# Fifteen early input blocks in place of nine in a two-layer transformer step

## The chip, the cores and the metric

The kernel runs on one core of one Trainium2 chip. The metric is the device time of one execution in microseconds (us), the median over several runs. The core has TensorE for matmuls (with a separate row for its weight loads), VectorE, ScalarE, GpSimd, and SyncE, whose queue issues plain transfers; 16 DMA engines move the data.

## The reference

The program applies two blocks to a sequence of 512 tokens of width 1024, all in float32. The first block mixes tokens by attention branches and then applies a PEER layer: for each token 128 experts are chosen, a row of `peer_u` and a row of `peer_v` (1024 numbers each) is fetched per expert, and the output is a weighted sum of the `peer_v` rows. The second block is a sparse attention and a feed-forward with a short causal convolution. Cut to what matters here:

```python
def peer_ffn(h, w_q, keys1, keys2, u_tab, v_tab):
    ...                                    # expert (128 per token), gate
        u = u_tab[eb]
        act = jax.nn.gelu(jnp.einsum('td,ted->te', hb, u), approximate=False)
        v = v_tab[eb]
        return jnp.einsum('te,ted->td', gb * act, v)

def conv_ffn(h, w_in, conv_w, conv_b, w_out):     # w_in: 1024 x 5632, D_FF = 2816
    u, v = jnp.split(h @ w_in, 2, axis=-1)
    u = conv(u, conv_w) + conv_b                  # causal, 3 taps along the sequence
    return (jax.nn.gelu(u, approximate=False) * v) @ w_out

def second_block(x, c, ...):
    ...
        x = x + gt_m * dsa_mixer(h, ...)
        h = rmsnorm(x, g_ffn[i]) * (1 + sc_f) + sh_f
        x = x + gt_f * conv_ffn(h, ...)
    return rmsnorm(x, g_final)
```

## The kernel before

The 512 tokens are four tiles of 128, numbered 0 to 3. The first block's attention part is done for tiles 0 and 1 and then 2 and 3. After that come, per tile, the PEER layer `peer(ti)` and the second block: its attention `dsa(t0, nt)`, and its feed-forward, `ffn_mod` (norm and modulation), `ffn_in` and `ffn_out`.

`peer(ti)` issues 128 gathers of `peer_u` rows (512 KB each: 128 tokens x 4 KB) from GpSimd (L618), a dot product on VectorE for each (L632), then 128 gathers of `peer_v` rows and a multiply-add on VectorE for each (L649). The rows use eight buffers in turn. One load of `ffn_norm_w` goes through SyncE into such a row buffer as well (L628).

The feed-forward's 2816 columns are 22 blocks of 128. One input block (`ffn_in`, L938 to L960) loads two 512 KB weight tiles through SyncE (L88, four buffers shared with `ffn_out`), multiplies them into two PSUM banks (L944, tag "mm", three banks), copies and convolves on ScalarE and VectorE (L947 to L954), and multiplies the halves into `gv` (L956). The cost in columns of a matmul is the number of tokens, 128 a tile; the weights are loaded anew for every pass over a block. The convolution needs the last two tokens of the tile before, kept in `fhalo`, so a block's tiles go in order.

The order of the work is set by priorities: a planner orders each engine's instructions once, when the program is built, by priority (mostly the order in the source) as their inputs and buffers come free. At run time each engine, and SyncE's queue, takes its instructions in that order. The lines around the change are L993 to L1015: attention of tiles 0 and 1 beside `peer(2)`; then, for tiles 0 and 1, the modulation and the first `EARLY` = 9 input blocks (256 columns); then the attention of tile 2, which needs `peer(2)`; then the first nine blocks for tile 2 alone (128 columns), the other 13 for tiles 0 to 2 together (384 columns), `ffn_out` of the three tiles (L978, three banks "mm"); `peer(3)` beside these at a lower place; the attention of tile 3 with a raised one; the feed-forward of tile 3, and `finish` (the last norm and the store, L986).

Of the kernel before, what the change touches and what calls it, by code (L numbers as in the profile page):

```python
# [26 lines left out]
LOW = -1e37  # L27
MARK = -3e38
GROUPS = ((0, 2, True), (2, 2, False))
EARLY = 9  # L30
LAG = 1
SPANS = [(a, sum(16 // (i + 1) for i in range(a)), 16 // (a + 1)) for a in range(8)]
NCAND = 50
# [26 lines left out]
def build(nc, tc, A, out):  # L60
# [872 lines left out]
    def ffn_in(F, t0, nt, fs):  # L933

        i0, _, hT, gv = F
        n = nt * 128
        cs = tok(t0 - i0, nt)
        for f in fs:  # L938
            bs = []
            for half in range(2):  # L940
                b = bank()[:, :n]
                w = w3(A["f_w_in"][half * NF + f], 8, tag="wf")
                for k in range(8):
                    PE.matmul(b, w[:, k, :], hT[:, k, cs], start=k == 0, stop=k == 7)  # L944
                bs.append(b)
            xb = sb.tile([128, NFG + 2], F32, name="xbf", bufs=2)[:, :n + 2]
            SC.activation(xb[:, 0:2], fhalo[:, f, :], AF.Copy)  # L947
            SC.activation(xb[:, 2:], bs[0], AF.Copy)
            SC.activation(fhalo[:, f, :], xb[:, n:n + 2], AF.Copy)
            y = sf("yf")[:, :n]  # L950
            SC.activation(y, xb[:, 0:n], AF.Copy, scale=fcw[:, f, 0:1])
            for c in (1, 2):
                V.scalar_tensor_tensor(y, xb[:, c:c + n], fcw[:, f, c:c + 1], y, op0=OP.mult, op1=OP.add)
            SC.activation(y, y, AF.Gelu, bias=fcw[:, f, 3:4])  # L954
            if len(gv) == 1:
                V.tensor_tensor(gv[0][:, f, cs], bs[1], y, op=OP.mult)  # L956
            else:
                V.tensor_tensor(y, bs[1], y, op=OP.mult)
                SC.activation(gv[0][:, f, cs], y, AF.Copy)
                V.tensor_tensor(gv[1][:, f, cs], y, gv[0][:, f, cs].bitcast(F32), op=OP.subtract)  # L960

    def ffn_mod(F, t0, nt):
        for ti in range(t0, t0 + nt):
            mod_T(ti, cols[4], cols[3], F[2][:, :, tok(ti - F[0])], "mm")

    def ffn_out(F):
        t0, nt, _, gv = F
        for q in range(2):
            qs = slice(q * 512, (q + 1) * 512)
            bs = [bank() for _ in range(nt)]  # L970
            for k0 in range(0, NF, 2):
                src = A["f_w_out"][q][:, k0 * 512:(k0 + 2) * 512]
                w = w3(src, 2, tag="wf") if len(gv) == 1 else wsplit(src, 2)
                for i in range(nt):
                    for k in range(2):
                        first, last = k0 + k == 0, k0 + k == NF - 1
                        if len(gv) == 1:
                            PE.matmul(bs[i], gv[0][:, k0 + k, tok(i)], w[:, k, :], start=first, stop=last)  # L978
                        else:
                            mm3(bs[i], [g[:, k0 + k, tok(i)] for g in gv], [t[:, k, :] for t in w], None, first, last)  # L980
            for i in range(nt):
                t = sf("yo")
                V.tensor_tensor(t, bs[i], gts[5][:, qs], op=OP.mult)
                V.tensor_tensor(x[:, t0 + i, qs], x[:, t0 + i, qs], t, op=OP.add)
# [13 lines left out]
    ffn_mod(F, 0, 2)  # L998
    ffn_in(F, 0, 2, range(EARLY))
    dsa(2, 1)  # L1000
    p0 = tc.cur_priority
    ffn_mod(F, 2, 1)
    ffn_in(F, 2, 1, range(EARLY))
    ffn_in(F, 0, 3, range(EARLY, NF))
    ffn_out(F)
# [105 lines left out]
```

## Time and profile before

| | us |
|---|---|
| median of 3 runs | 2645.74 |
| range of the runs | 2644.31 to 2646.25 |
| profiled execution | 2659.27 |
| its span in the trace | 2657.5 |
| TensorE matmul busy | 2075.4 (78%) |
| VectorE busy | 1983.3 (75%) |
| GpSimd busy | 1182.3 (44%) |
| ScalarE busy | 830.5 (31%) |

The profile is of one execution. Its first part gives busy times, its second cuts the span into 40 slices of 66.4 us, its fourth is the chain of work that ended last, its fifth the costliest groups of instructions. Other answers of the trace give busy times by stretch, instructions by line, the timeline and the transfers. Busy shares are means over stages with different limits, so a stage is read by its own rows.

### The profile page before, as it was taken

To read this page: it belongs to the slowest core of one execution; us is meant where nothing else is said; L and a number is where in the kernel's file an instruction comes from. 1 tells how busy PE (TensorE), PEld (TensorE's weight loads), DVE (VectorE), ACT (ScalarE), POOL (GpSimd) and SP (SyncE) were. 2 spreads that over 40 slices of the span, in tenths; PEclk is the share of its full clock that TensorE was granted. 3 is DMA by queue.
4 is the path that set the end of the run, shared out by engine and by line. 5 is a ranking of instruction groups with operands and counts; after the bars stand their busy time and mean duration, and the time that the engine had idled before them with its cause. 6 is when DMAs were issued, how large, how long until landed. Compare 5 with 4: busy or idle time off the path is not lost. (4 is left out here: it accounts for less than half of the span.)

```text
span 2657.5 us, 31631 instructions
## 1 busy us (share of the span) xinstructions
PE 2075.4 (78%) x10438; PEld 1572.0 (59%) x10438; DVE 1983.3 (75%) x4068; ACT 830.5 (31%) x1827; POOL 1182.3 (44%) x1092
## 2 busy tenths in 40 slices
PE   5988999888987899886766655658053789898997
PEld 5887889577776677764622234637032565444795
DVE  6873333289799999778899589887989778875235
ACT  5655563223344344111211123411022221003444
POOL 0111100024656877555566755665765557860000
PEclk9999999998999999898899967879566999999999
DMA  8852335368979799999998999999999999992286
GB/s 272 280 174 67 95 105 184 118 241 315 372 284 339 261 358 387 386 409 406 404 325 307 356 390 372 350 381 407 400 384 339 399 409 409 395 409 87 80 287 235
DMA packets 230596, 808.85 MB, mean 304 GB/s; under 512 B 26617, under 2 KB 34081, under 8 KB 230433
## 3 DMA queue, kind: packets, MB, share of 16 engines
q0 software_dynamic: 147456, 536.94, 53.1%
q1 hardware_dynamic: 82976, 269.90, 28.5%
q8 instruction: 83, 1.36, 0.2%
q14 instruction: 81, 0.66, 0.1%
HBM read 802.52 MB, written 4.21 MB: 304 GB/s over the span
## 5 line engine op out<-in xcount | busy, mean ns | idle before, releaser
L618 POOL DMA_INDIRECT row<-peer_u,exi x512 | 489.6, 956 | 682.2 <-DVE ix L552 269.2
L618 POOL DMA_INDIRECT row<-peer_v,exi x512 | 609.7, 1191 | 245.1 <-issue 102.8
L632 DVE CUSTOM_DVE_ANT_0 row<-row,h 128x1024 f32<-128x1024 f32 x512 | 613.6, 1213 | 78.8 <-DMA row<-peer_u,exi 77.8
L649 DVE SCALAR_TENSOR_TENSOR x<-row,pw,x 128x1024 f32<-128x1024 f32 x448 | 584.7, 1305 | 83.1 <-DMA row<-peer_v,exi 77.6
L944 PE MATMUL bmm<-hTf,w 128*128 128x128 f32 (+2 forms) x1696 | 317.3, 347 | 19.7 <-DMA w<-f_w_in 9.4
L944 PEld LDWEIGHTS bmm<-hTf,w 128*128 128x128 f32 x1696 | 246.4, 191 | 89.9 <-DVE gv L956 10.1
L271 PE MATMUL bmm<-hT,w 128*128 128x256 f32 x1168 | 273.9, 385 | 2.9 <-ACT xb L307 1.3
L271 PEld LDWEIGHTS bmm<-hT,w 128*128 128x128 f32 x1168 | 221.6, 193 | 42.7 <-issue 10.0
L647 PE MATMUL acc<-row,dgw 128*128 128x512 f32 x256 | 130.2, 636 | 81.4 <-DMA row<-peer_v,exi 67.6
L351 POOL TENSOR_TENSOR Lb<-LT,clevels_b 128x512 f32<-128x512 f32 x56 | 71.0, 1271 | 268.9 <-DVE LT L342 209.3
L99 DVE TENSOR_TENSOR wrowb<-w,wrowa 128x1024 fp32r<-128x1024 f32 x95 | 118.3, 1250 | 76.8 <-ACT wrowa L98 76.7
L105 PE MATMUL bmm<-hTh,wrowa 128*128 128x256 f32 x584 | 169.8, 292 | 2.9 <-ACT hTh L209 2.8
L106 PE MATMUL bmm<-hTl,wrowa 128*128 128x256 f32 x584 | 170.9, 293 | 0.7 <-DVE hTl L210 0.7
L107 PE MATMUL bmm<-hTh,wrowb 128*128 128x256 f32 x584 | 168.6, 289 | 0.8 <-DVE wrowb L99 0.8
L647 PEld LDWEIGHTS acc<-row,dgw 128*128 128x128 f32 x256 | 45.6, 197 | 165.3 <-issue 90.5
L978 PE MATMUL bmm<-w,gv 128*128 128x512 f32 x264 | 118.8, 604 | 10.3 <-DVE gv L956 8.6
L98 ACT ACTIVATE wrowa<-w 128x1024 fp32r<-128x1024 f32 x95 | 100.3, 1058 | 81.7 <-PE bmm L106 36.3
L271 PE MATMUL bmm<-h2T,w 128*128 128x256 f32 x512 | 120.6, 390 | 0.0
L105 PEld LDWEIGHTS bmm<-hTh,wrowa 128*128 128x128 f32 x584 | 111.8, 192 | 5.8 <-ACT hTh L209 3.2
L106 PEld LDWEIGHTS bmm<-hTl,wrowa 128*128 128x128 f32 x584 | 111.5, 191 | 4.5 <-issue 3.1
L107 PEld LDWEIGHTS bmm<-hTh,wrowb 128*128 128x128 f32 x584 | 111.6, 191 | 4.4 <-issue 3.1
L723 PE MATMUL bat<-dgm,x 128*128 128x128 f32 x64 | 15.1, 431 | 121.3 <-ACT dgm L719 121.3
(399 smaller groups left out, 3577.6 us busy)
## 6 DMA issues: line engine op xcount, KB each, us to landing
w<-w_in SPq DMA_DIRECT2D x144, 512.0 KB, 5.7
w<-f_w_in SPq DMA_DIRECT2D x106, 512.0 KB, 6.7
x<-ada_wT SPq DMA_DIRECT2D x48, 512.0 KB, 4.5
w<-f_w_out SPq DMA_DIRECT2D x44, 512.0 KB, 5.0
w<-w_br SPq DMA_DIRECT2D x32, 512.0 KB, 5.5
w<-peer_wq SPq DMA_DIRECT2D x32, 512.0 KB, 6.8
w<-a_w_o SPq DMA_DIRECT2D x24, 512.0 KB, 6.7
w<-w_out SPq DMA_DIRECT2D x16, 512.0 KB, 5.1
```

Source lines behind the costliest of these rows:

```text
L98: SC.activation(hi, w, AF.Copy)
L99: V.tensor_tensor(lo, w, hi.bitcast(F32), op=OP.subtract)
L105: PE.matmul(b, w[0], r[0], start=start, stop=False)
L106: PE.matmul(b, w[0], r[1], start=False, stop=False)
L107: PE.matmul(b, w[1], r[0], start=False, stop=stop)
L271: PE.matmul(b, w[:, k, :], rhs[k // 4][:, k % 4, :], start=k == 0, stop=k == 7)
L618: G.indirect_dma_start(out=t, out_offset=None, in_=tab, in_offset=bass.IndirectOffsetOnAxis(ap=ix[:, j:j + 1], axis=0))
L632: V.tensor_tensor_reduce(out=u, in0=u, in1=h2, scale=1.0, scalar=0.0, op0=OP.mult, op1=OP.add, accum_out=act[:, j:j + 1])
L647: PE.matmul(acc[:, q:q + 512], dg, v[:, q:q + 512], start=j == onpe[0], stop=j == onpe[-1])
L649: V.scalar_tensor_tensor(xt, v, w[:, j:j + 1], xt, op0=OP.mult, op1=OP.add)
L944: PE.matmul(b, w[:, k, :], hT[:, k, cs], start=k == 0, stop=k == 7)
L978: PE.matmul(bs[i], gv[0][:, k0 + k, tok(i)], w[:, k, :], start=first, stop=last)
```

## The change

One number: `EARLY` goes from 9 to 15. Blocks 9 to 14 of tiles 0 and 1 (256 columns) are issued ahead of the attention of tile 2; the same blocks of tile 2 (128 columns) are issued behind it on their own; the pass over three tiles (384 columns) keeps seven blocks, 15 to 21, in place of 13. What is computed does not change.

```diff
--- before.py
+++ after.py
@@ -27,7 +27,7 @@
 LOW = -1e37
 MARK = -3e38
 GROUPS = ((0, 2, True), (2, 2, False))
-EARLY = 9
+EARLY = 15
 LAG = 1
 SPANS = [(a, sum(16 // (i + 1) for i in range(a)), 16 // (a + 1)) for a in range(8)]
 NCAND = 50
```

`EARLY` is read in three places: `ffn_in(F, 0, 2, range(EARLY))`, `ffn_in(F, 2, 1, range(EARLY))` and `ffn_in(F, 0, 3, range(EARLY, NF))`, with `NF` = 22.

## Rows read from the trace of the kernel before

**Rows 1.** Page, second part: TensorE's busy tenths in 40 slices

```profile
PE   5988999888987899886766655658053789898997
```

**Rows 2.** Page, fourth part: the chain that ended last, by line

```profile
DMA row<-peer_v,exi 6%; DVE row L632 4%; POOL row L618 3%; PE bmm L944 3%; PE bat L921 2%; DVE x L649 1%; PE bat L877 1%; DVE acc L818 1%; DVE m L817 1%; DMA w<-f_w_out 1%; DMA w<-f_w_in 1%; PE bmm L978 1%; DMA w<-a_w_o 1%; PE bat L754 1%; DMA row<-peer_u,exi 1%
```

**Rows 3.** By stretch: length, PE, PEld, DVE, ACT, POOL busy (count), PEclk, DMA share, GB/s

```profile
1793.00:1853.00 60.00, 56.24 (x257) 48.16 (x255) 48.70 (x56) 13.19 (x42) 32.59 (x33) 1.00 1.03 407
1862.00:1900.00 38.00, 0.00 (x0) 0.00 (x0) 37.00 (x31) 0.00 (x0) 29.03 (x28) 0.50 1.02 403
1947.00:2105.00 158.00, 88.22 (x405) 62.50 (x405) 136.85 (x293) 39.11 (x91) 87.84 (x94) 0.77 0.97 367
2000.00:2050.00 50.00, 10.00 (x44) 7.28 (x45) 50.00 (x117) 6.11 (x14) 28.17 (x30) 0.61 0.95 351
```

**Rows 4.** Groups by line, 1793 to 1853: count, busy us, mean ns, idle before

```profile
L649 DVE SCALAR_TENSOR_TENSOR x<-row,pw,x 128x1024 f32<-128x1024 f32 x33 | 42.4, 1284 | 11.3 <-DMA row<-peer_v,exi 11.0
...
L953 DVE SCALAR_TENSOR_TENSOR yf<-xbf,f_conv,yf 128x256 f32<-128x256 f32 x16 | 7.6, 477 | 0.0
...
L956 DVE TENSOR_TENSOR gv<-bmm,yf 128x256 f32<-128x256 f32 x7 | 2.9, 417 | 0.0
```

**Rows 5.** Timeline, 1862 to 1951: start, length, engine, line, count, [idle before]

```profile
1862.44 76.56 DVE L649 SCALAR_TENSOR_TENSOR x<-row,pw,x 128x1024 f32<-128x1024 f32 x58
1932.43 0.33 SPq L628 DMA_DIRECT2D row<-ffn_norm_w  x1
...
1950.44 3.79 PE L723 MATMUL bat<-dgm,x 128*128 128x128 f32 x16 [98.64 <-ACT dgm L719]
```

**Rows 6.** By stretch, behind the attention of tile 2, columns as in rows 3

```profile
2110.00:2153.00 43.00, 34.33 (x280) 32.17 (x280) 31.27 (x71) 11.98 (x44) 18.88 (x21) 1.00 1.02 407
2153.00:2279.00 126.00, 123.24 (x389) 72.22 (x388) 107.33 (x119) 22.99 (x58) 88.09 (x71) 1.00 1.03 409
2305.00:2391.00 86.00, 84.16 (x191) 36.80 (x192) 68.72 (x58) 0.00 (x0) 58.62 (x46) 0.98 1.01 399
```

**Rows 7.** Timeline of SyncE's queue, from 2277, columns as in rows 5

```profile
2277.36 101.06 SPq L88 DMA_DIRECT2D w<-f_w_out  x18
...
2413.57 29.50 SPq L88 DMA_DIRECT2D w<-f_w_out  x2
...
2503.30 15.78 SPq L88 DMA_DIRECT2D w<-f_w_in  x4
```

**Rows 8.** Page, fifth part: matmuls of the joint `ffn_out`

```profile
L978 PE MATMUL bmm<-w,gv 128*128 128x512 f32 x264 | 118.8, 604 | 10.3 <-DVE gv L956 8.6
```

**Rows 9.** Timeline, 2391 to 2545: end of `peer(3)`; from tile 3's attention to its feed-forward

```profile
2391.79 1.28 DVE L649 SCALAR_TENSOR_TENSOR x<-row,pw,x 128x1024 f32<-128x1024 f32 x1 [1.25 <-DMA row<-peer_v,exi]
...
2501.39 17.33 PE L978 MATMUL bmm<-w,gv 128*128 128x512 f32 x40
...
2507.72 0.40 ACT L719 ACTIVATE dgm<-cmats,rrmm 128x128 f32<-128x128 f32 x1 [0.80 <-DVE rrmm L146]
...
2518.55 1.95 PE L723 MATMUL bmm<-dgm,x 128*128 128x128 f32 x16
...
2520.55 5.91 PE L944 MATMUL bmm<-hTf,w 128*128 128x128 f32 x48
...
2532.11 13.05 PE L944 MATMUL bmm<-hTf,w 128*128 128x128 f32 x114 [0.52 <-DVE yf L958]
```

**Rows 10.** Timeline: tile 2's norm for the feed-forward

```profile
2107.01 3.54 PE L723 MATMUL bmm<-dgm,x 128*128 128x128 f32 x16 [8.91 <-ACT dgm L719]
```

**Rows 11.** By stretch, around rows 10, columns as in rows 3

```profile
2105.00:2110.00 5.00, 2.99 (x14) 3.00 (x15) 4.64 (x12) 0.40 (x1) 3.52 (x4) 0.50 1.02 409
```

**Rows 12.** Chain in order of time, two pieces in the attention of tile 3

```profile
2418.25 0.86 PE bmm L978 x2
...
2460.01 2.63 PE bmm L978 x4
```

**Rows 13.** Issued transfers, 1783 to 1853: KB each, us to landing

```profile
w<-f_w_in SPq DMA_DIRECT2D x18, 512.0 KB, 7.1
```

## The prediction

> **What bounds the kernel now.** I read four views in this order. The page's slices [rows 1] show TensorE's busy share fall to nothing in slice 29 (1860 to 1927 us) and stay low in 30 and 31: there is a hole in its work. The page's chain [rows 2] names row transfers, VectorE's dot products and GpSimd's gathers ahead of any matmul: the end is set by the expert gathers (peer), then by the work behind them. The table by stretch [rows 3] says why: in 1793 to 1900 the DMA engines move 403 and 407 GB/s, and where they move less VectorE is full, so a row is late because bytes or VectorE are in its way. Last, the timeline, for the hand-overs. The order of the end is: peer(2) accumulates x[2] until some 1943; dsa(2) has its matmuls from 1950 [rows 5] to some 2105; ffn_in and ffn_out of tiles 0 to 2 run beside peer(3); then dsa(3), ffn_in and ffn_out of tile 3, alone. TensorE's hole lies between the ninth early block and the first matmul of dsa(2) at 1950.44, 98.6 us [rows 5]. It costs nothing by itself: TensorE waits there for peer(2), which is set by rows.
>
> **Step A: six more early blocks, in the hole.** Each block is 32 matmul instructions of 256 columns with two 512 KB weight loads, two L953 and one L956 on VectorE, and some six short ScalarE operations. 257 such matmuls took 60 us [rows 3], 7.47 us a block, so six take 44.8 us: 1852 to 1897, inside the hole with 53 us to spare. TensorE's own cost is nil, covered by peer(2). ScalarE is busy 13 us of 60 in the same stretch [rows 3] and doesn't bind. The loads do. Loads go from 18 + 18 + 26 + 44 (early, tile 2 alone, the joint pass, tile 3) = 106 to 30 + 30 + 14 + 44 = 118: twelve more, 6.29 MB, and all twelve fall in this place, because behind dsa(2) it is 18 + 26 = 44 before and 30 + 14 = 44 after. Price by the pace of rows: with early blocks beside them 33 accumulations fit into 60 us [rows 4], 1.82 us each; without, 58 took 76.56 us [rows 5], 1.32 each. In 44.8 us that is 24.6 in place of 33.9; 9.3 lost x 1.32 = **+12.3 us** for peer(2)'s end. Upper bound: all 6.29 MB at 407 GB/s [rows 3], 15.5 us. Lower bound: VectorE's added work alone, 6 x (2 x 0.477 + 0.417) = 8.2 us [rows 4], for VectorE is full without blocks (37.0 of 38 us, rows 3). I take 12.3, the pace of this same pair of streams. dsa(2) starts by that much later. Its 158 us don't change, and peer(3), whose rows are bound by VectorE there (50.0 of 50 us, rows 3) and by bytes behind it, ends later by as much.
>
> The Trainium skill, DMA: Bandwidth & Descriptors (Queues, rings and completion order), has each DMA engine take packets from the queues with work in turn. Were both queues never empty, rows would have half of 407 GB/s; the rows here show that they keep 33 x 524,288 B in 60 us = 288 GB/s, since TensorE asks only for two loads in 7.5 us. What the even split would cost is a rival below.
>
> **Step B: behind dsa(2).** Six blocks leave the joint pass and enter tile 2's pass. 280 matmuls of 128 columns took 43 us, 4.9 us a block; 389 of 384 columns took 126 us, 10.4 us a block [rows 6]. So the input blocks end 6 x (10.4 - 4.9) = 33 us sooner after dsa(2). This isn't on the path, which is peer(3) here; but it brings loads forward. Before, 18 of the 22 joint f_w_out loads are issued ahead of peer(3)'s end, the rest after it, and tile 3's first four f_w_in from 2503 on [rows 7]. After, all 22 are, and some of the four f_w_in too as buffers come free. Each load ahead of the last row costs 524,288 B / 409 GB/s [rows 6] = 1.28 us. Bounds: 0 (the last rows go at 1.32 us anyway [rows 5], if loads slip between) to 8 x 1.28 = 10.3; I take six, **+7.7 us**. Extra VectorE work of the split (one more pass of three short operations a block) is beside 107 busy of 126 us [rows 6] and isn't counted again.
>
> **Step C: the tail.** Of ffn_out's 264 matmuls, 118.8 us [rows 8], 84 us lie in 2305 to 2391 [rows 6] and little ahead of that; some 30 us are left over, as pieces inside dsa(3) and 17.3 us at 2501 [rows 9]. 33 us sooner after dsa(2), and B's 7.7 us of longer peer(3), leave room for all of it ahead of dsa(3), which waits for peer(3)'s last accumulation, at 2393 now [rows 9]. Then:
> The scaling of tile 3's norm is ready on ScalarE at 2508.1, and its matmuls (L723) start at 2518.55, held by the left-over (same queue, and all three banks "mm") [rows 9]: -10.4. Without that work TensorE stands idle there for some 6 us, and after 8.9 us of idle the same 16 matmuls took 3.54 us at a granted clock of 0.50, 1.2 GHz [rows 10, 11], against 1.95 here at 1.00, 2.4 GHz: +1.6.
> The first 80 matmuls of ffn_in(3) take from 2520.55 to 2532.11, 11.6 us, among finish's ScalarE and VectorE work; the next 114 took 13.05 [rows 9], so 9.2 would do: -2.4.
> Pieces of L978 on the chain of dsa(3), 2.63 and four of 0.86 us like the one shown [rows 12]: up to -6; some fall into waits, I take -4.
> finish(0, 3) moves into dsa(3): three L990, of L649's kind and size (1.28 us, rows 4), and short operations beside VectorE's top-k chain: 0 to +6, I take +4.
> Together **-11.2 us**, bounds -18.8 (no clock loss, all gains, finish free) to -2.8 (finish wholly on the chain, no gain from pieces nor at ffn_in's start).
>
> **Sum:** +12.3 + 7.7 - 11.2 = +8.8 us. The profiled execution, 2657.5 of span and 2659.27 in all, would become 2668.1; it lies 0.5% over the median of the runs, 2645.74, and a term shrinks by no more than that, so the forecast is **2654.5 us**, slower by 0.33%. Ends of all terms: 8.2 + 0 - 18.8 = -10.6 and 15.5 + 10.3 - 2.8 = +23.0; the forecast's own range, without all ends at once, is 2646 to 2664.
>
> **Rivals.**
> 1. The delay is made good in dsa(2) (faster). From 1947 to 2105 the DMA moves 367 GB/s [rows 3]; (409 - 367) x 158 us = 6.6 MB of room, enough for the twelve loads' worth of rows. If rows of peer(3) use it, A is 0 for peer(3)'s end, B is the four f_w_out, 5.1, and C stands: -6.1, **2639.6**. It decides as soon as VectorE in dsa(2) has more than 12 us free for rows. Against it: VectorE was busy 136.9 of 158 us, and full where the DMA was least used [rows 3]; those rows were there and waited for VectorE.
> 2. SyncE's queue. The load of ffn_norm_w for peer(3) stands behind the early loads in SyncE's order and waits for a row buffer until 1932.43 [rows 5]. If some of the twelve new loads are ordered behind it, they start after peer(2), and the matmuls of dsa(2) are queued behind the blocks that need them: two blocks late are 15 us and a load's 7.1 us [rows 13], some +20 on the forecast, **2674**. Against: at two loads in 7.47 us the last leaves by 1897, 35 us before that wait ends.
> 3. The even split: rows get 204 GB/s while blocks run, 2.58 us each, 17.4 rows in 44.8 us, 16.5 lost x 1.32 = 21.8 in place of 12.3: **2664**. It is the skill's rule above. Against: the 288 GB/s measured, at two loads in 7.5 us.
> 4. The change doesn't clear the tail: the left-over of ffn_out stays queued between dsa(3) and L723, because its order on TensorE follows a plan and not the time; A and B with a third of C: +16.3, **2662**.
>
> **Chances.** Forecast 0.52, rival 1 0.25, rival 2 0.06, rival 3 0.07, rival 4 0.10. About 0.2% (5.3 us) is what a measurement of this kernel can tell from no change. Of the forecast's 0.52, 0.05 falls below that, 0.20 within, 0.27 above; of rival 1, 0.22 faster and 0.03 within; rivals 2 to 4 are slower. So faster 0.27, same 0.23, slower 0.50. The range reaches below rival 1 and above rivals 3 and 4, and leaves out most of rival 2 and the far ends: 2635 to 2668.
>
> **What would show it.** A: L944 of 256 columns without a gap to about 1897, the run of 58 back-to-back accumulations cut to some 33, dsa(2)'s first L723 at about 1963 in place of 1950. B: 15 blocks of 128 columns and seven of 384, ffn_out begun some 20 us sooner, all 22 f_w_out issued before the last row, peer(3)'s last accumulation near 2413. C: no L978 behind that, L723 of tile 3 some 7 us behind the last L921, and from peer(3)'s end to the end of the span about 253 us in place of 264. Wrong would be: dsa(2) later but peer(3) not (rival 1), a gap in the early blocks with SyncE waiting for a row (rival 2), rows at more than 2.2 us beside them (rival 3), L978 behind the last L921 (rival 4).

## The result and the profile after

The changed kernel takes 2677.11 us (median of 4 runs, 2669.14 to 2684.28), the kernel before, run beside it, 2645.99 us (4 runs, 2644.31 to 2651.53): 1.0113 times as long, 95% interval 1.0078 to 1.0148. Two more comparisons, on two chips, gave 1.0103 (1.0083 to 1.0124) and 1.0090 (1.0071 to 1.0110). The sign was the forecast's (slower by 0.33%, chance 0.50), the size was not: the time lies above the range of 2635 to 2668 us. The execution profiled after took 2669.14 us, 2667.3 of it the span, the fastest of its runs; that of before took 2659.27.

To compare the two, I cut each span at the same nine events, all read from timelines: the first early L944, the first L723 of `dsa(2)`, of tile 2's feed-forward, of `dsa(3)` and of tile 3's feed-forward, the end of `peer(3)`'s last L649, the end of the last L921, and the first and last L944 of tile 3. The stretch ahead of the first early block has the same instructions in the same order in both kernels and varies from run to run (1775.0, 1785.5 and 1788.6 us in three profiles of the changed kernel, 1783.6 and 1785.4 in two of before), so it is left out; "the rest" is the 5.7 us between `peer(3)` and `dsa(3)` and what stands behind the last L944. Mean of the three profiles against mean of the two, in us:

| stretch | before | after | measured | predicted |
|---|---|---|---|---|
| first early block to `dsa(2)` | 166.5 | 180.4 | +13.9 | +12.3 |
| `dsa(2)` to tile 2's feed-forward | 155.7 | 154.9 | -0.8 | 0 |
| from there to the end of `peer(3)` | 285.8 | 294.5 | +8.7 | +7.7 |
| `dsa(3)`, first L723 to the end of the last L921 | 102.8 | 113.7 | **+11.0** | **0** (-4 +4) |
| wait ahead of tile 3's L723 | 17.0 | 6.6 | -10.4 | -10.4 |
| L723 to the first L944 | 2.0 | 3.6 | +1.6 | +1.6 |
| `ffn_in(3)` | 85.7 | 83.1 | -2.6 | -2.4 |
| the rest | 56.6 | 56.8 | +0.2 | 0 |
| sum | | | +21.6 | +8.8 |

Seven of eight rows came within 1.6 us. One row holds the mistake.

**Step A, right.** The table by stretch of the kernel after (columns as in [rows 3]) and then its timelines (columns as in [rows 5]):

```profile
1784.00:1895.00 111.00, 99.88 (x451) 84.43 (x449) 89.27 (x101) 21.81 (x70) 60.95 (x60) 1.00 1.02 406
1900.00:1940.00 40.00, 0.00 (x0) 0.00 (x0) 38.31 (x33) 0.60 (x2) 29.00 (x29) 0.50 1.02 403
1953.00:2108.00 155.00, 87.08 (x405) 61.50 (x405) 136.32 (x289) 38.65 (x91) 87.63 (x92) 0.76 0.97 371
```

```profile
1850.09 44.69 SPq L88 DMA_DIRECT2D w<-f_w_in  x12
1938.22 0.33 SPq L628 DMA_DIRECT2D row<-ffn_norm_w  x1
...
1887.25 7.17 PE L944 MATMUL bmm<-hTf,w 128*128 128x256 f32 x32 [0.49 <-DVE gv L956]
1956.09 3.79 PE L723 MATMUL bat<-dgm,x 128*128 128x128 f32 x16 [61.67 <-ACT dgm L719]
...
1903.90 40.90 DVE L649 SCALAR_TENSOR_TENSOR x<-row,pw,x 128x1024 f32<-128x1024 f32 x31
```

The fifteenth block ends at 1894.4, TensorE's hole has shrunk from 98.64 us [rows 5] to 61.67, and of the 58 rows in a row 31 are left. In the 111 us beside the blocks VectorE does 60 accumulations (L649), 1.85 us apart, as in [rows 4] (1.82). SyncE has the twelve loads out long before its next wait.

**Step B, right, by another count.** SyncE's queue behind `dsa(2)`, to hold against [rows 7]:

```profile
2152.06 92.60 SPq L88 DMA_DIRECT2D w<-f_w_in  x26
2249.50 119.73 SPq L88 DMA_DIRECT2D w<-f_w_out  x22
2374.05 15.78 SPq L88 DMA_DIRECT2D w<-f_w_in  x4
```

(The view starts at 2150; earlier loads of `f_w_in` aren't in it.) All 22 `f_w_out` and the four `f_w_in` of tile 3 go out ahead of `peer(3)`'s last row at 2404.6: eight loads brought forward, not the six that I took, at 8.7 / 8 = 1.09 us each, not 1.28.

**Step C, wrong in one place.** The end of `dsa(3)` and the feed-forward behind it, to hold against [rows 9], and the groups of ScalarE in 2410 to 2524:

```profile
2520.33 3.70 PE L921 MATMUL bat<-w,oT 128*128 128x512 f32 x8 [1.08 <-DMA w<-a_w_o]
2530.66 3.73 PE L723 MATMUL bmm<-dgm,x 128*128 128x128 f32 x16 [6.63 <-ACT dgm L719]
2534.22 9.16 PE L944 MATMUL bmm<-hTf,w 128*128 128x128 f32 x80
```

```profile
L141 ACT ACT_TABLE_LOAD x4 | 5.1, 1283 | 0.1
L142 ACT ACT_TABLE_LOAD x4 | 5.1, 1283 | 0.1
L152 ACT ACTIVATE row<-x 128x1024 f32<-128x1024 f32 x3 | 3.1, 1045 | 0.0
```

No L978 stands behind the last L921 any more, the wait is 6.63 us, the L723 pay the low clock, and the first 80 matmuls of `ffn_in(3)` take 9.2 us in place of 11.6: all as predicted. But `dsa(3)` itself has grown by 11 us, and ScalarE has three L152 and three pairs of table loads more in it: the three row norms of `finish(0, 3)`. (L141 is a norm's logarithm, L142 its exponential; an ACT_TABLE_LOAD is the load of a function table that stands ahead of them.) ScalarE's timeline shows where the first of the three stands:

```profile
2422.22 1.28 ACT L141 ACT_TABLE_LOAD   x1
2423.51 0.20 ACT L141 ACTIVATE ryd<-rmd 128x2 f32<-128x2 f32 x1
2423.62 1.04 ACT L152 ACTIVATE row<-x 128x1024 f32<-128x1024 f32 x1
2424.57 0.19 ACT L152 ACTIVATION_READ_ACCUMULATOR row<-x 128x1 f32 x1
2424.77 1.28 ACT L142 ACT_TABLE_LOAD   x1
2426.07 0.20 ACT L142 ACTIVATE ryd<-ryd 128x2 f32<-128x2 f32 x1
2426.29 1.28 ACT L141 ACT_TABLE_LOAD   x1
2427.58 0.20 ACT L141 ACTIVATE ry<-rm 128x1 f32<-128x1 f32 x1
2427.80 1.28 ACT L142 ACT_TABLE_LOAD   x1
2429.10 0.20 ACT L142 ACTIVATE ry<-ry 128x1 f32<-128x1 f32 x1
2430.19 0.47 ACT L768 ACTIVATE cq<-bat,rrd 128x256 f32<-128x256 f32 x1 [0.89 <-DVE ckv L767]
```

`ryd` is the attention's own norm. L152 of `finish` stands between its logarithm (L141) and its exponential (L142), 1.2 us; then `finish`'s own pair of table loads takes 3 us. VectorE, whose order is fixed as well, has the sums of both norms interleaved and waits for `finish`'s before it gives the attention its own:

```profile
2426.70 0.17 DVE L145 TENSOR_SCALAR rtd<-rtd 128x2 f32<-128x2 f32 x1
2429.33 0.16 DVE L143 TENSOR_TENSOR rt<-ry 128x1 f32<-128x1 f32 x1 [2.47 <-ACT ry L142]
2429.41 0.15 DVE L146 TENSOR_TENSOR rrd<-ryd,rtd 128x2 f32<-128x2 f32 x1
```

The other two norms of `finish` stand further on, beside the scores (L813) and in the middle of the top-k chain (L817, L818), and VectorE waits for each in the same way:

```profile
2441.16 0.16 DVE L143 TENSOR_TENSOR rt<-ry 128x1 f32<-128x1 f32 x1 [2.54 <-ACT ry L142]
...
2453.40 0.16 DVE L143 TENSOR_TENSOR rt<-ry 128x1 f32<-128x1 f32 x1 [2.51 <-ACT ry L142]
```

The last step of each norm, L990, isn't in `dsa(3)` at all: the first one starts at 2535.7, behind the last L921.

```profile
L990 DVE SCALAR_TENSOR_TENSOR row<-x,rr,gfin x4: 1277/1279/1284, 2535.7 to 2662.0; 128x1024 f32<-128x1024 f32 x4
```

### The profile page after: what moved, and what is told of

It is laid out like the page before. It is cut to its first block, busy times and chain, and to the rows that moved or that the text cites. A ratio compares the mean times of both kernels' runs of the same rounds, so it can differ in the third digit from the quotient of the medians.

```text
span 2667.3 us, 32100 instructions
## 1 busy us (share of the span) xinstructions
PE 2088.4 (78%) x10630; PEld 1603.2 (60%) x10630; DVE 1983.5 (74%) x4086; ACT 838.4 (31%) x1859; POOL 1182.7 (44%) x1092
## 5 line engine op out<-in xcount | busy, mean ns | idle before, releaser
L649 DVE SCALAR_TENSOR_TENSOR x<-row,pw,x 128x1024 f32<-128x1024 f32 x448 | 585.7, 1307 | 93.2 <-DMA row<-peer_v,exi 88.0
L944 PE MATMUL bmm<-hTf,w 128*128 128x128 f32 (+2 forms) x1888 | 321.8, 330 | 30.8 <-DVE gv L956 12.9
L944 PEld LDWEIGHTS bmm<-hTf,w 128*128 128x128 f32 x1888 | 269.7, 193 | 82.4 <-DVE gv L956 18.1
L98 ACT ACTIVATE wrowa<-w 128x1024 fp32r<-128x1024 f32 x95 | 100.2, 1058 | 82.6 <-PE bmm L106 34.8
L978 PE MATMUL bmm<-w,gv 128*128 128x512 f32 x264 | 116.2, 600 | 8.5 <-DVE gv L956 6.4
L271 PEld LDWEIGHTS bmm<-h2T,w 128*128 128x128 f32 x512 | 100.2, 201 | 14.2 <-DVE h2T L212 0.7
```

Of the source, the lines that this page charges most:

```text
L98: SC.activation(hi, w, AF.Copy)
L271: PE.matmul(b, w[:, k, :], rhs[k // 4][:, k % 4, :], start=k == 0, stop=k == 7)
L649: V.scalar_tensor_tensor(xt, v, w[:, j:j + 1], xt, op0=OP.mult, op1=OP.add)
```

## Experiments

The theory at this point: A and B as predicted; `finish`'s norms inside `dsa(3)` cost 9 to 11 us; the left-over matmuls taken out of `dsa(3)` give nothing. Rivals: the norms are beside the chain and `dsa(3)` grew by the TensorE clock; the loads don't set A or B; the differences between chips and runs make up the rest.

The kernel before takes 2654.31 us on the chip of r0, r1, e1 and e2 (19 runs), 2707.25 on that of e3 to e6 (22 runs, where the lead-in takes 1814 us and `dsa(2)` to tile 2's feed-forward 173), 2652.52 on that of r2, e7, e8 and e9 (29 runs), and 2652.97 beside e10 to e12, which ran on the chip of r0 again (23 runs). So whole times are compared within a chip; the other stretches are alike on all.

**r0 and r1: both kernels again.** No edit.

> The kernel before under a label of its own, for a second profile of it on this chip. Both theories: no difference beyond 3 us from the kernel before. If lead-ins differ by chance, its first early matmul starts near 1775 and not at 1783.6; if they don't, at 1783 again.

> The changed kernel as it is, timed in five rounds against the kernel before on one chip. The two profiles at hand are 9.8 us apart in span (2667.3 and 2657.5), the medians 31 us. Theory (the cost is local: early blocks to the end 18 us longer, and the profile of before had a lead-in some 9 us longer than the one of after by chance): the medians here lie 15 to 22 us apart. Rival (the stretch behind the early blocks itself differs from run to run by 10 us or more): 25 to 35 us apart, and this profile's stretches differ from the first one's by that much.

Before: 1.0007 (0.9994 to 1.0021) against itself; the change 2680.52 us, 1.0103 (1.0083 to 1.0124). The medians lie 23.9 us (r0) to 26.2 us (the 19 runs beside them) apart, more than the 15 to 22 of the theory; but the rival isn't borne out either, for the change takes 893.2 us from the first early block to the end here and took 892.3 in its first profile. The lead-in of before came at 1785.4, not near 1775, and it is the change that has 1775.0 in one profile and 1785.5 in another. The two spans differ by 23.1 us, and 23.0 of that lie in the stretches of the table (+13.8, +0.4, +9.6, +10.4, -10.4, +1.5, -1.7, -0.6).

**e1: `finish`'s norms held until `x[3]` is complete.** The L152 get a scale of 1.0 that is worked out from tile 3's `x`.

```
-    finish(0, 3)
+    one = sm.tile([128, 1], F32, name="one")
+    V.tensor_scalar(one, x[:, 3, D - 1:D], 0.0, 1.0, op0=OP.mult, op1=OP.add)
+    finish(0, 3, scale=one)
```

> The changed kernel, with the norm of finish(0, 3) made to wait (through a scale column worked out from x[3]) until the attention of tile 3 is done, as it is in the kernel before. Theory (finish's three norms with their table loads on ScalarE lie in the chain of dsa(3) and make it 10.9 us longer): dsa(3), first L723 to last L921, falls from 113.8 to 103 to 106 us, ffn_in(3) starts up to 4 us later behind it, and the time is 4 to 9 us less than that of the changed kernel. Rival (TensorE's clock, granted 0.5 to 0.9 in dsa(3) since no ffn_out work fills its gaps): dsa(3) stays at 110 or more and the time is the same.

`dsa(3)` took 104.1 us, 9.3 less than the 113.4 of the two profiles of the change known by then: the norms are what lengthened it. But now they stand around tile 3's own norm: the wait ahead of L723 is 10.6 us in place of 6.6, L944 comes 5.9 us behind it in place of 3.6, and `ffn_in(3)` takes 89.5. The four stretches add up to 210.1 us, not less than the 206.9 of r1. By whole times e1 was 2672.82 us against 2680.52, 7.7 less and inside the expected 4 to 9; its profiled execution, 2679.59, was the slowest of its runs, so the place of those 7.7 us isn't seen.

**e2: the twelve loads of step A left out.** The six added blocks take activations as weights (and read them as `w[:, k, 0:128]`, in e3 and e9 too).

```
-                w = w3(A["f_w_in"][half * NF + f], 8, tag="wf")
+                w = hT if nt == 2 and f >= 9 else w3(A["f_w_in"][half * NF + f], 8, tag="wf")
```

> The changed kernel without the loads of the six added early blocks: their matmuls take the activations as weights (so these six blocks of tiles 0 and 1 are left out and something else of the same cost stands there). Theory (the twelve loads' bytes displace rows): the stretch from the first early matmul to the first matmul of dsa(2) falls from 181.1 to 173 to 176 us, where VectorE's own added work (8.2 us on 166.8) is left, and the time by 5 to 8 us. Rival (VectorE's work and not the loads sets it): 180 or more, time the same. Rival (loads alone): 167 to 169, time 12 to 14 us less.

From the first early block to `dsa(2)` 172.0 us, 8.4 less than the 180.4 of the change; the whole 2665.35 us, 15.2 less, twice the 5 to 8 us that the theory gave it and over the 12 to 14 of the second rival. The stretches of its profile hold 8.6 of the 15.2; where the rest lies isn't seen. Of A's 13.9 us the loads' bytes are 8.4, and 5.5 remain for the blocks without loads, less than the 8.2 us of VectorE's added work. A is made by both, as the pace of rows had it.

**e3: the twelve loads behind `dsa(2)` left out** (the same edit for `t0 == 2 and f >= 9`).

> Left out: the 12 loads of feed-forward weights behind the second attention (blocks 9 to 14 of the third tile); their matmuls take activations as weights instead, so the amount of arithmetic is the same and the output is not the reference's. Theory (the loads share the link with the gather that the end of the second tile's feed-forward to the third waits for): the stretch from the last matmul of the second tile's feed-forward to the end of the third tile's peer stage falls from about 294.6 us to about 279 us, 12 times 1.28 us less, and the whole by about 15 us. Rival (that stretch is set by VectorE and the gather's own pace): the stretch stays within 2 us of 294.6 us, and the whole within 3 us of the change.

The stretch to `peer(3)`'s end took 280.2 us, 14.3 less than the change's 294.5, 1.19 us per load. The rival (unchanged, VectorE sets it) is out. On this chip the whole is 1.0034 (1.0021 to 1.0047) times before; the change itself wasn't run on it, so the 15 us expected of the whole can only be judged by that ratio against 1.0090 to 1.0113.

**e4: twelve early blocks.** `EARLY = 12`.

> Twelve early blocks in place of fifteen (before: nine). Theory (two terms in proportion, one that is there whole once the left-over matmuls are cleared ahead of the third attention, because the planner then puts the norms of the final stage inside its ScalarE chain): the stretch of the early blocks and the second attention +7 us against before, the stretch to the end of the third peer stage +4 us, the third attention 111 to 114 us in place of 103, the wait of the first matmul behind it about 7 us in place of 17: in all 8 to 15 us over before. Rival (all in proportion to the number of blocks): third attention 108 us, in all about 13 us over before.

The early stretch 173.8 us (+7.4), to `peer(3)`'s end 290.6 (+4.8), both half of the change's. `dsa(3)` took 112.0 us, as with fifteen, and not the rival's 108; the wait behind it is 6.6. The whole: 1.0051 (1.0032 to 1.0069), +12.6 us. So the cost in `dsa(3)` isn't in proportion to the blocks; it is there in full with twelve, where, as with fifteen, no left-over matmul stands behind the last L921. Ten and eleven weren't tried.

**e5 and e6: the norms held until block 12 of `ffn_in(3)`,** in the change and in the kernel before. As e1, with `F[3][0][:, 12, 127:128]` in place of `x[3]`'s column.

> The change, with the norm of the final stage of tiles 0 to 2 held until block 12 of the third tile's last feed-forward matmuls. Theory: the third attention takes about 104 us in place of 113, the wait of the first matmul behind it 6.6 us, the delay of the first feed-forward block behind that 3.6 us (5.9 with the earlier gate), the last feed-forward 82 to 90 us; in all 8 to 15 us under the change, still 8 to 15 us over before. Rival (what the third attention gives back is lost in the stage behind it): the sum of these four stretches stays at 205 to 209 us, and the whole within 4 us of the change.

> The kernel before with the same gate on the final stage as the run just named. Theory: the final stage of the kernel before stands in the wait behind its third attention, where TensorE clears left-over matmuls, so that moving it gains 0 to 4 us at most; the third attention stays at 103 us. Rival (the norms also cost the kernel before): third attention or the wait behind it shorter by 5 us or more.

e5: `dsa(3)` 102.2 us, the wait 6.6, L944 3.6 behind it, `ffn_in(3)` 88.1. The four add up to 200.5 us against 207.0 in the change (mean of three), 6.5 less: of the 11.5 us that leave `dsa(3)`, 5 come back in `ffn_in(3)`. That is between theory (8 us or more) and rival (4 or less). The whole is 1.0062 (1.0044 to 1.0080) times before, +15.9 us, just over the expected 8 to 15; the change had 1.0090 to 1.0113. The clock as the cause is out: `dsa(3)` has the same 453 records of matmuls as in the change, with no left-over among them, and takes what it takes in the kernel before. ScalarE's timeline shows the same place as above without `finish`:

```profile
2479.26 1.28 ACT L141 ACT_TABLE_LOAD   x1
2480.56 0.20 ACT L141 ACTIVATE ryd<-rmd 128x2 f32<-128x2 f32 x1
2480.78 1.28 ACT L142 ACT_TABLE_LOAD   x1
2482.07 0.20 ACT L142 ACTIVATE ryd<-ryd 128x2 f32<-128x2 f32 x1
2483.68 0.47 ACT L768 ACTIVATE cq<-bat,rrd 128x256 f32<-128x256 f32 x1 [1.41 <-DVE ckv L767]
```

From the start of the table load to L768 it is 4.42 us here, 7.97 in the change: the first norm costs 3.55 us. The places of all three show in the same way, in us from the first L723 of `dsa(3)`, with one norm more ahead of each VectorE line:

| start of | change | e5 | difference | added by this norm |
|---|---|---|---|---|
| table load of the attention's norm, on ScalarE | 11.95 | 11.44 | 0.51 | |
| L767, `ckv` | 19.40 | 15.34 | 4.06 | 3.55 |
| first MAX8, L817 | 37.62 | 30.46 | 7.16 | 3.10 |
| L819, `sel` | 64.44 | 54.73 | 9.71 | 2.55 |
| end of the last L921 | 113.76 | 102.24 | 11.52 | |

So the three norms make 9.2 of the 11.5 us. Of the other 2.3, 0.5 lies ahead of the first norm and 1.08 is the wait of L921 for `a_w_o` that stands in the timeline of the change above and not in e5; what made them isn't shown.

e6: 1.0006 (0.9992 to 1.0019), `dsa(3)` 102.8, the wait 17.0, as in the kernel before. There the norms cost nothing that holding them gives back.

**e9: the three causes out at once.** e5 with the edits of e2 and e3: no load that the change moves, norms held.

> Left out: all 24 loads that the change moves ahead (12 ahead of the second attention, 12 behind it); their matmuls take activations as weights, so the output is not the reference's. The norm of the final stage is held until block 12 as well. Theory (the three costs add): against before the stretch of the early blocks +5.5 us, the stretch to the end of the third peer stage -6 us (12 loads fewer there than the change, 6 fewer than before), the third attention 0, the first matmul behind it -10.4 us, the delay of the feed-forward block +1.6 us: about 9 us under before (5 to 13), so 28 to 36 us under the change. Rival (one stretch hands its gain to the next): less than 20 us under the change.

2647.93 us, 33.0 less than the change on the same chip (r2) and inside the expected 28 to 36: the costs of the loads and of the norms add, no stretch hands its gain to the next. Against before it is 0.9977 (0.9960 to 0.9994), -4.6 us, a little less than the -5 to -13 expected (24 loads are out where the change has twelve and eight more ahead of the last rows, so that it has fewer than before: 54 against 58 in the third stretch); `ffn_in(3)` took 87.0, as in e5.

**r2: the change a third time,** beside e7 to e9.

> The change itself, for its time beside the three runs after it on one chip. Theory and rival alike: 18 to 28 us over before.

2680.95 us, 1.0090 (1.0071 to 1.0110), 28.4 us over before, just outside the expected 18 to 28. Its profile gives +25.0 against r0's stretches.

**e7, e8, e11, e12: fewer early blocks than before.** `EARLY = 7`, `5`, `7` again and `8`.

> Seven early blocks, where before has nine. Theory (the two terms that grow with the number of blocks also shrink with it): the stretch of the early blocks and the second attention 14.0 / 6 x 2 = 4.7 us shorter than before, the stretch to the end of the third peer stage 8.8 / 6 x 2 = 2.9 us shorter, 14 more left-over matmuls behind the third attention at 0.21 us (full clock) to 0.43 us (half clock) = 3.0 to 6.0 us later: 1.6 to 4.6 us under before. Rival (nine stands at the bottom already, since the wait behind the third attention and the clock take back more): 0 to 5 us over before.

> Five early blocks, where before has nine. Theory as for seven: 9.3 us and 5.9 us shorter in the two stretches, 30 more left-over matmuls behind the third attention, 6.4 to 12.9 us later: 2 to 9 us under before. Rival: the two stretches do not shrink below those of before, and the whole is 5 to 13 us over before.

> Seven early blocks again. Theory: 2 to 5 us under before, third attention 100 us, the wait behind it 29 us, as in the run of seven before this. Rival (that gain was chance): within 1 us of before.

> Eight early blocks. Theory (the cost per block of the two stretches against 14 records of left-over matmuls at 0.43 us): between nine and seven, the stretch of the early blocks 164 us, the stretch to the end of the third peer stage 280 to 284 us, the wait behind the third attention 23 us: 0 to 4 us under before. Rival (the step from nine to seven comes at once with eight, because one load less fits ahead of the end of the third peer stage): the stretch to the end of the third peer stage at 279 us or less.

| early blocks | first block to `dsa(2)` | loads issued, tile 2's feed-forward to `peer(3)`'s end | that stretch | `dsa(3)` | wait behind | whole against before |
|---|---|---|---|---|---|---|
| 5 | 155.2 | 53 | 274.2 | 100.2 | 42.8 | 1.0001 (0.9989 to 1.0014) |
| 7 | 161.7, 160.9 | 55 | 278.6, 279.0 | 100.2 | 29.0 | 0.9983 (0.9969 to 0.9997), 0.9993 (0.9981 to 1.0006) |
| 8 | 164.1 | 57 | 281.6 | 101.6 | 23.0 | 0.9995 (0.9977 to 1.0013) |
| 9 | 166.5 | 58 | 285.8 | 102.8 | 17.0 | 1 |
| 12 | 173.8 | 62 | 290.6 | 112.0 | 6.6 | 1.0051 |
| 15 | 180.4 | 66 | 294.5 | 113.7 | 6.6 | 1.0090 to 1.0113 |

The third stretch follows the number of loads, with 54 in e3 (280.2) and e9 (281.3) too: a straight line through all seventeen profiles has 1.31 us per load, about the 524,288 B / 409 GB/s = 1.28 of the prediction; 8 comes out at 281.6 us, where the rival of a step asked for 279 or less. The wait behind `dsa(3)` grows by 12.0 us from nine to seven blocks, where I had expected 3.0 to 6.0: the timeline of e7 shows 68 records of L978 there in place of 40 [rows 9], at 29.35 / 68 = 0.43 us each. I had counted 14 where 28 stand, and taken 0.43 for the price at half the clock; here it is the price at a granted clock of 1.00.

```profile
2469.51 8.32 PE L921 MATMUL bat<-w,oT 128*128 128x512 f32 x19
2477.67 29.35 PE L978 MATMUL bmm<-w,gv 128*128 128x512 f32 x68
2506.85 1.95 PE L723 MATMUL bmm<-dgm,x 128*128 128x128 f32 x16
```

Seven blocks were faster than both kernels in one comparison, by 0.17%, and no different from before in the other (2648.98 and 2649.06 us against 2652.52 and 2652.97). Five give all of it back, where 2 to 9 us less than before had been expected, and eight are as nine.

**e10: matmuls put back into `dsa(3)`.** e5 with 30 matmuls whose result nothing reads, of L978's width. Each matmul has two records in the trace. Twelve of them (24 records) stand inside `dsa(3)`, each within about 1 us of the place where the kernel before has one of its twelve left-over ones; two more stand at its very end and not, as expected, among the others.

```
-    ffn_out(F)
+    ffn_out(F); db = bank()
+    [PE.matmul(db, gts[2][:, 0:128], gts[5][:, 0:512], start=True, stop=True) for k in range(30)]
```

> The change with the norms held until block 12, and 30 matmuls added that compute nothing which is used (as wide as the left-over ones, results dropped): 16 stand ahead of the third attention, 14 inside it, nearly where the kernel before has its 12 left-over pairs. Theory (the left-over matmuls inside the third attention cost what the higher clock gives back): the third attention stays at 100 to 104 us and the granted clock in it rises from 0.91 to 0.95 or more. Rival (they cost 4 us there and the clock has nothing to do with it, so that something else took back what their removal should have brought): the third attention becomes 106 us or more.

`dsa(3)` took 102.1 us, the same as e5's 102.2 without them. The table by stretch, columns as in [rows 3], of before, of the change, of e5 and of e10:

```profile
2399.00:2502.00 103.00, 98.08 (x479) 66.19 (x480) 41.49 (x100) 37.32 (x82) 0.00 (x0) 0.96 0.16 52
```

```profile
2410.00:2524.00 114.00, 94.05 (x453) 66.67 (x453) 42.61 (x114) 49.33 (x101) 0.00 (x0) 0.87 0.13 42
```

```profile
2468.00:2570.00 102.00, 90.52 (x453) 64.63 (x453) 41.19 (x99) 37.22 (x82) 0.00 (x0) 0.92 0.14 47
```

```profile
2419.00:2521.00 102.00, 97.08 (x478) 64.97 (x478) 41.26 (x100) 37.30 (x82) 0.00 (x0) 0.97 0.14 47
```

With 25 more records TensorE is busy for 6.6 us more, the mean granted clock is 0.97 in place of 0.92 (1.00 is 2.4 GHz, 0.50 is 1.2), and the stretch is as long as without them. The whole is 1.0085 (1.0056 to 1.0114) times before, of two runs. So the left-over matmuls cost `dsa(3)` nothing, and their removal could give nothing; the rival (106 us or more) is out. The clock moved as the theory wants it; that it and nothing else balances the account isn't shown, since no run could hold the clock fixed.

## Why the prediction was wrong, step by step

- **Bound, right.** Rows set the end, and what shares the link with them or delays VectorE is paid: e2, e3 and the table of loads show it load by load.
- **A, +12.3 against +13.9.** Price by the pace of rows with and without blocks beside them. e2 splits it into 8.4 us of loads and 5.5 us of the rest; neither end alone (bounds 15.5 and 8.2) would have done. That SyncE and the matmuls have room was right.
- **B, +7.7 against +8.7.** The mechanism was right (loads brought ahead of the last row). It was eight loads and not six at 1.09 us and not 1.28; that the two errors nearly cancel is luck.
- **C, -11.2 against -0.4: here it failed.** Three of its five terms came as worked out (-10.4, +1.6, and -2.6 for -2.4). The two that were to cancel didn't. `finish(0, 3)` inside `dsa(3)` was taken at +4 (0 to +6) for VectorE's L990 and "short operations". The term named the wrong engine and the wrong operation: no L990 stands in `dsa(3)`, but each norm puts an L152 of 1.04 us and two table loads of 1.28 us on ScalarE, in the middle of the attention's own chain. VectorE's order then makes the attention wait for the exponential of each of `finish`'s norms (2.47, 2.54 and 2.51 us above). 11.5 us leave `dsa(3)` when they are held (113.7 to 102.2, e5). The rows were there to be read in the trace of before, in ScalarE's timeline:

```profile
2516.77 1.06 ACT L152 ACTIVATE row<-x 128x1024 f32<-128x1024 f32 x1 [8.65 <-DVE x L984]
...
2519.65 1.28 ACT L141 ACT_TABLE_LOAD   x1
...
2521.17 1.28 ACT L142 ACT_TABLE_LOAD   x1
```

  There `finish` waits for L984, the last addition of `ffn_out`, which the left-over matmuls hold up until 2517, and so falls beside tile 3's L723 and feed-forward. Take the left-over away and that wait ends in `dsa(3)`. A norm with its own table loads is 1.04 + 2 x 1.28 = 3.6 us of ScalarE, and three are 10.8 as an estimate from these rows; measured they cost 3.55 + 3.10 + 2.55 = 9.2 us (e5), on an engine that the prediction hadn't looked at in that stage (ScalarE busy for 37.32 of 103 us before, 49.33 of 114 after). The removed L978 were taken at -4; they give nothing (e5 against before: -0.6 us; e10). (The prediction's counts of matmuls are counts of records, two for each: the 264 L978 are 132 matmuls, the 80 L944 are 40. Its times come from the same rows and don't change by it.)
- **Base.** With the two terms of C put at +11 and 0, the sum is 12.3 + 7.7 - 10.4 + 1.6 - 2.4 + 11 = +19.8, 2665.5 us. What remains to 2677.11 is 11.6 us: 2.6 are the early stretch and B. For the rest the base counts too. The 2645.74 that the sum was made on is the median of three runs, and the 2645.99 beside the change has the same three in it and one more, so it is no second measurement; later the kernel before had medians of 2654.31 (19 runs) and 2652.52 (29 runs), with the change 26.2 and 28.4 us over them and not 31.1. That still leaves some 5 to 7 us over the 21.6 of the profiled stretches. Only a few executions of each kernel were profiled, and the time in the others can't be divided into stretches. That rest stays open.
- **Rival 1** (made good in `dsa(2)`): no. That stretch is only 0.8 us shorter, and `peer(3)` ends later by A and B together (13.9 - 0.8 + 8.7 = 21.8 us from the first early block). VectorE is busy for 136.3 of 155 us there, as before.
- **Rival 2** (SyncE's queue): no. The twelve loads are out by 1894.8, and SyncE reaches its wait 43 us ahead of `ffn_norm_w`.
- **Rival 3** (even split): not beside the early blocks. Rows come at 1.85 us each there, not 2.58, and of the bytes in 1785 to 1895 the gather's queue (q0) moved two thirds, the weights' queue (q1) one third (packets, MB, share of the engines' time):

```profile
q0 software_dynamic: 8191, 29.83, 68.3%
q1 hardware_dynamic: 4059, 14.79, 33.9%
```

  The split does occur behind `dsa(2)`, where the change has tile 2's blocks and SyncE issues a load about every 2.6 us. From 2153 to 2175:

```profile
q1 hardware_dynamic: 1225, 4.48, 51.3%
q0 software_dynamic: 1232, 4.48, 50.9%
```

  By the Trainium skill, DMA: Bandwidth & Descriptors (Queues, rings and completion order), each DMA engine takes packets in turn from the queues that it has work for. The trace agrees, with 4.48 MB each where loads follow without a pause; beside the early blocks, two loads in 7.4 us are 142 GB/s, less than half of the 406 that the engines move there.
- **Rival 4** (left-over stays): no, L978 ends at 2389, ahead of `dsa(3)`. With twelve blocks (e4) some of it is still inside `dsa(3)`, none behind it.

The Trainium skill, ScalarE: Activation LUTs (Table sets: the hidden batching unit), says that a logarithm and an exponential in succession need one table load, since one set has both. The trace agrees where the kernel loads that set itself (L125, L133, L1012): 19 of the 28 norms of the kernel before, all that stand ahead of the first GELU of the feed-forward (L954, 1793.8 us) and the very last one, have no load ahead of L141 nor ahead of L142. The last one:

```profile
2651.29 0.20 ACT L141 ACTIVATE ry<-rm 128x1 f32<-128x1 f32 x1 [0.22 <-DVE rm L140]
2651.53 0.20 ACT L142 ACTIVATE ry<-ry 128x1 f32<-128x1 f32 x1
```

In between, from that GELU on, there is a load ahead of L141 and another ahead of L142: in the change for every norm, in the kernel before eight pairs for nine norms. So the pair of loads that the three norms pay isn't a property of the norm: it took 3.0 us from load to exponential in `dsa(3)` (2426.29 to 2429.30) and takes 0.4 us above. No run tried to load the set ahead of `dsa(3)`, so what of the 9.2 us that would give back is open.

## What to carry to other kernels

When a change clears the work that stood in front of a waiting stage, ask which other work was held up behind it, and price that on every engine it uses, by rows of the stage it will now fall into: here a 10.4 us gain freed three norms, and the next chain became 11 us longer. Look at an engine's table loads before calling a norm short, and at whether the operation that you price stands in that stage at all. Work that is off the path for TensorE can still be paid for through the link it loads from; count the loads that go out ahead of the last row, and take about a load's bytes over the link's rate for each (1.09 to 1.31 us measured here, 1.28 by bytes). A wait filled with left-over work is not waste while what fills it would be paid elsewhere.

## What the runs showed of the hardware

- Twelve matmuls of 512 columns more or fewer inside an attention of 102 us don't change its length; the granted clock goes from 0.92 to 0.97 with them (e5, e10), and to 0.98 in e7, where `dsa(3)` takes 100.2 us.
- An ACT_TABLE_LOAD took 1283 ns, with 0.1 us of idle time ahead of four of them in all. A norm with one load ahead of its logarithm and one ahead of its exponential holds ScalarE for 3.0 us even when its operands have one column; with the common set loaded before, 0.4 us.
- In 22 us in which weight loads followed without a pause, they and the gather moved 4.48 MB each; at two weight loads in 7.4 us, the gather kept 29.83 of the 44.6 MB of both in 110 us.
- The kernel before took 2652 to 2654 us on two chips and 2707 us on a third. Of those 55 us some 30 lie ahead of the first early block and 18 between `dsa(2)` and tile 2's feed-forward (155 and 173 us). Why that chip is slower, no run here tells.
